# Feed-forward's first quarter: squares on ScalarE, and the first halves of the first two output units ahead of both second halves

## The chip, the cores and the metric

One core of a Trainium2 chip runs the whole program. It has a matrix engine (TensorE, PE in the profile), VectorE (DVE), ScalarE (ACT), GpSimd (POOL) and SyncE (SP), which here only issues DMAs. Each engine takes its instructions in a fixed order that was set when the program was built, and an instruction that waits holds up all that stand behind it on its engine. The metric is the time of one execution on the device, in microseconds (us), as the median of several runs.

## The reference, cut to what matters

Two layers over 640 tokens (128 of a context, 512 latent) and a width of 1024. Each layer has a mixing part (attention and a state-space scan), and behind it a feed-forward part with 4096 hidden units:

```
h = RMSNorm(x) * (1 + scale2) + shift2
x += gate2 * W2 relu(W1 h)^2
```

The change touches only this feed-forward part, in both layers. Its scale, shift and gate differ between context tokens and latent tokens, so operations on a 128x640 tile are often done in two pieces, 128x128 and 128x512.

## The kernel before, in words

The values live transposed: 128 features on the partitions, 640 tokens along the free dimension. A float32 product is made from three: each operand is split into a high part (rounded to the matrix engine's fp32r) and a low part (what is left), and high by high, low by high and high by low are added up in the accumulator. For weights the parts are `wh` and `wl`: ScalarE casts the high one (L1782) and VectorE subtracts for the low one (L1783). For the hidden values they are `uh` and `ul`: a cast on ScalarE (L307) and a subtraction on VectorE (L308).

The hidden units are worked through in four quarters, `q` = 0 to 3, of 8 hidden tiles each. In a quarter, first the **first product** makes 8 hidden tiles of 128x640; then the **second product** runs over 8 output units m = 0 to 7 (128 features of x each), and every unit adds what this quarter's 8 hidden tiles give it. The change is all in q = 0.

- *First product of q = 0.* Tiles 0 and 1 are made together (`early`), tiles 2 to 7 one after the other (`plain`): two `block`s of 24 matmuls on the accumulator `fm`, then `squared`. That multiplies by the norm's factor on VectorE (`un`, L533), copies a small bias vector (`bsh`, L538, ScalarE), adds the bias on ScalarE in two pieces (L1877 and L1878), takes max(v, 0) * v on VectorE (`u`, L1871), and splits it (`uh` on ScalarE, `ul` on VectorE).
- *Second product of q = 0.* Every unit has two blocks. The first reads hidden tiles 0 to 3, the second tiles 4 to 7, which end with the last one made. One block is 4 tiles x 3 products x 2 halves of the tokens, 24 matmuls in 12 groups of two. After its second block a unit's accumulator goes to `residual` (L546), three VectorE operations that add it to x, and so free the accumulator. There are two accumulators of this kind, so unit m + 2 can't begin before unit m's residual is done; `ffx`, the first accumulator of the next quarter, is one of the same two.
- *Beside it.* While the second product of q = 0 runs, VectorE and ScalarE make the operands of the later quarters from x (`expanded`: `nh` L1826 and L1828, `ta` and `tb` L1847, `e`, `eh`, `el`). In layer 0 `fill.step()` puts in work for layer 1's modulation vectors, VectorE multiplications with a throw-away output called `junk` (L428). GpSimd forms sums of weight tiles for the next quarter (`wS`, L1769).
- *Order.* `Stream` hands weights to the blocks in the order of its list `src`, one entry for each block; DMAs run up to seven cost units ahead (an entry costs two here), and the split of the weights is made one block ahead. The order of the instructions on each engine is worked out by the framework's scheduler from the data's dependences and its own estimates, so a change in the code can move instructions elsewhere too.

Of the kernel before, what the change touches and what calls it, by code (L numbers as in the profile page):

```python
# [14 lines left out]
AF = mybir.ActivationFunctionType  # L15
ALU = mybir.AluOpType
# [8 lines left out]
NCTX = 128  # L25
# [80 lines left out]
def build(nc, tc, a, ctx):  # L106
    vec, act, pool, pe = nc.vector, nc.scalar, nc.gpsimd, nc.tensor
# [11 lines left out]
    @contextlib.contextmanager  # L119
    def after(ins):  # L120

        with ExitStack() as st_:
            for i_ in ins:
                st_.enter_context(tc.issue_after(i_.ins))
            yield
# [7 lines left out]
    def nm(s):  # L133
        uid[0] += 1
        return f"{s}_{uid[0]}"
# [7 lines left out]
    def G(shape, dt=F32, name="g"):  # L143

        assert size(shape) <= GW, shape
        return sp.tile(list(shape), dt, tag="G", name=nm(name), bufs=NG)

    def X(shape, dt=F32, name="t"):

        assert size(shape) <= 648, shape  # L150
        return sp.tile(list(shape), dt, tag="X", name=nm(name), bufs=NX)

    def Y(shape, dt=F32, name="t"):

        assert size(shape) <= 512, shape
        return sp.tile(list(shape), dt, tag="Y", name=nm(name), bufs=NXS)
# [4 lines left out]
    def PA(name="pa"):  # L161
        return psp.tile([P, 2, 512], F32, tag="pa", name=nm(name), bufs=2)
# [147 lines left out]
    def halves(ps):  # L310
        return [(ps[:, h, :HT], slice(h * HT, (h + 1) * HT)) for h in range(2)]
# [1430 lines left out]
    class Stream:  # L1742
# [12 lines left out]
        def unit(self, name, cost):  # L1755

            self.src += [(cost, lambda h=h: self.raw(name, h)) for h in range(2)]

        def pair(self, n1, n2):

            box = {}

            def fetch():
                for key, (n, h) in (("11", (n1, 0)), ("21", (n2, 0)), ("22", (n2, 1)), ("12", (n1, 1))):
                    box[key] = self.raw(n, h)
                for key, x0, x1, op in (("S1", "21", "22", ALU.add), ("S2", "S1", "11", ALU.subtract),
                                        ("S3", "11", "21", ALU.subtract), ("S4", "12", "S2", ALU.subtract)):
                    box[key] = Y([P, 512], name="wS")
                    pool.tensor_tensor(out=box[key], in0=box[x0], in1=box[x1], op=op)  # L1769

            def take(key):
                if not box:
                    fetch()
                return box[key]

            self.src += [(1, lambda key=key: take(key)) for key in ("11", "12", "S2", "S1", "S3", "S4", "22")]
# [26 lines left out]
    def block(out, w, xh, xl, first, last, on=False):  # L1803

        hi, lo = w
        with after(done):
            for i in range(4):
                wh, wl = hi[:, i * P:(i + 1) * P], lo[:, i * P:(i + 1) * P]
                for w_, x_, s_, e_ in ((wh, xh[i], first and i == 0, False), (wh, xl[i], False, False),
                                       (wl, xh[i], False, last and i == 3)):  # L1810
                    for o, ts in out:
                        mm = pe.matmul(o, w_, x_[:, ts], start=s_, stop=e_, skip_group_check=on)  # L1812
        done[:] = [mm]
# [38 lines left out]
    def feed_forward(l, nrm, fill):  # L1852
        W = Stream(l)
        for q in range(4):
            if q == 0:
                for m in range(8):
                    W.unit(f"f1_{q}_{m}", 2)
            else:
                for m in range(4):
                    W.pair(f"f1_{q}_{m}", f"f1_{q}_{m + 4}")  # L1860
            for m in range(8):
                W.unit(f"f2_{q}_{m}", 2)
        ex = {n: ([], []) for n in ("B11", "B21", "B22", "T1", "T2", "T3", "T4")}
        expand = expanded(l, nrm, ex)
        nxt = Norm()
        full = slice(0, HT)

        def hidden(v, m, uh, ul):

            u = X([P, T], name="u2")  # L1870
            vec.scalar_tensor_tensor(out=u, in0=v, scalar=0.0, in1=v, op0=ALU.max, op1=ALU.mult)  # L1871
            uh[m], ul[m] = G([P, T], F32R, name="uh"), G([P, T], F32R, name="ul")
            evac_split(uh[m], ul[m], u)

        def squared(m, ps, uh, ul):
            t_, b = nrm.out(ps)
            act.activation(out=t_[:, :NCTX], in_=t_[:, :NCTX], func=AF.Identity, bias=b[:, 0:1])  # L1877
            act.activation(out=t_[:, NCTX:], in_=t_[:, NCTX:], func=AF.Identity, bias=b[:, 1:2])  # L1878
            hidden(t_, m, uh, ul)

        def early(uh, ul):

            ps = [PA("fm") for _ in range(2)]
            ws = [[W.next() for _ in range(2)] for _ in range(2)]
            for k in range(KD):
                with after(nrm.last):
                    if k == 4:
                        nrm.rows()
                    if k == 5:
                        nrm.spread()  # L1890
                for w, p_ in zip(ws, ps):
                    hi, lo = w[k // 4]
                    fm(zhalves(p_), hi[:, (k % 4) * P:], lo[:, (k % 4) * P:], nrm.zh, nrm.zl, [k], 0, KD - 1)
            for m, p_ in enumerate(ps):
                squared(m, p_, uh, ul)

        def plain(m, uh, ul):

            ps = PA("fm")
            for h in range(2):  # L1900
                block(zhalves(ps), W.next(), nrm.zh[4 * h:4 * h + 4], nrm.zl[4 * h:4 * h + 4], h == 0, h == 1)
            squared(m, ps, uh, ul)

        def pair(ms, uh, ul):
            px, pz, py = PA("ffx")[:, 0, :HT], PB("ffz")[:, :HT], PB("ffy")[:, :HT]
            v1, v2_ = X([P, 2, HT], name="v1"), X([P, 2, HT], name="v2")
            sy = Y([P, HT], name="sy")

            def go(out, n, first):
                block([(out, full)], W.next(), *ex[n], first, True, not first)  # L1910

            go(px, "B11", True)
            act.copy(out=v1[:, 0], in_=px)
            go(pz, "B21", True)
            vec.tensor_tensor(out=v1[:, 0], in0=v1[:, 0], in1=pz, op=ALU.add)
            go(px, "T2", False)
            act.copy(out=v1[:, 1], in_=px)
            go(py, "T1", True)
            act.copy(out=sy, in_=py)
            go(px, "T3", False)  # L1920
            vec.tensor_tensor(out=v2_[:, 1], in0=sy, in1=px, op=ALU.add)
            go(py, "B22", False)
            vec.tensor_tensor(out=v1[:, 1], in0=v1[:, 1], in1=py, op=ALU.add)
            go(px, "T4", False)
            act.copy(out=v2_[:, 0], in_=px)
            for v, m in zip((v1, v2_), ms):
                hidden(v.rearrange("p h t -> p (h t)"), m, uh, ul)

        mark(f"{l}ff")
        for q in range(4):  # L1930
            uh, ul = [None] * 8, [None] * 8
            if q == 0:
                early(uh, ul)

                for m in range(8):
                    mark(f"{l}ff")
                    if m >= 2:
                        plain(m, uh, ul)
                    fill.step()
            else:  # L1940
                for m in range(4):
                    mark(f"{l}ff")
                    pair((m, m + 4), uh, ul)
                load_x(xsave, 0)
            for m in range(8):
                mark(f"{l}ff")
                if q and m + 1 < KD:
                    load_x(xsave, m + 1)
                if q == 0 and m < 4:
                    next(expand)  # L1950
                ps = PA("fm")
                for h in range(2):
                    block(halves(ps), W.next(), uh[4 * h:4 * h + 4], ul[4 * h:4 * h + 4], h == 0, h == 1)
                residual(l, 5, m, ps)
                nc.sync.dma_start(a["yT"][:, m] if l == DEPTH - 1 and q == 3 else xsave[:, m], x[m])
                if q == 3:
                    if l + 1 < DEPTH:
                        mark(f"{l + 1}norm1")
                        nxt.scaled(l + 1, 0, m)
                        nxt.square(m)  # L1960
                if q or m >= 4:
                    fill.step()
        while fill.live:
            fill.step()
        return nxt
# [43 lines left out]
    for l in range(DEPTH):  # L2009
        f0 = Part(ada_stream(ADA_S) if l == 0 else ada_rows([(1, 3), (1, 4)]), 1)  # L2010
        n2 = mixing(l, nrm, f0, *((second, raws0) if l == 0 else ()))
# [126 lines left out]
```

## Time and profile before

| | |
|---|---|
| median of 3 runs | 1838.08 us (1836.33 to 1839.86) |
| profiled execution | 1835.58 us |
| its span | 1833.8 us |
| mean granted TensorE clock | 0.968 |
| TensorE busy | 95% of the span |
| VectorE busy | 72% |
| ScalarE busy | 45% |
| GpSimd busy | 25% |

The profiled execution is 2.50 us under the median, and its span 1.78 us shorter than its own time. A share is a mean over the whole span: an engine with a share of 72% can still be full in one stretch, and it is the stretch that counts for a change in one place.

### The profile page before, as it was taken

The numbers are of one execution on the slowest core, as the hardware profiler recorded it, in microseconds if no ns is written. First come the engines' busy times: TensorE is split into PE (matmuls) and PEld (weight loads), VectorE is DVE, ScalarE is ACT, GpSimd is POOL, SyncE is SP. The second block draws the span as 40 slices with busy tenths as digits, with TensorE's granted clock in tenths as the row PEclk, the third lists the DMA queues.
The fourth block names the chain that finished last, engine by engine and source line by source line (L and its number), as shares of the span: only waits on it lengthen the run. The fifth ranks groups of instructions, "written<-read, shape, count | busy, mean of one in ns | idle before, by whom it ended". The sixth has DMA issues, their size and how long they took to land. (4 is left out here: it accounts for less than half of the span.)

```text
span 1833.8 us, 31636 instructions
## 1 busy us (share of the span) xinstructions
PE 1739.1 (95%) x11692; PEld 1616.5 (88%) x11692; DVE 1314.4 (72%) x2738; ACT 828.1 (45%) x1732; POOL 464.3 (25%) x538
## 2 busy tenths in 40 slices
PE   6899998999999999999997999889999999999999
PEld 4797865878999999999997987679989999999998
DVE  6784776744678987786776779988677877465562
ACT  6553446644445351433544533387535445243340
POOL 1424532101210322303135244541003031130400
PEclk8899989999999999999998999789999999999999
DMA  9123122351143447264541322112424242524341
GB/s 337 56 71 101 52 63 80 101 181 64 41 158 107 141 129 231 90 224 133 169 148 45 92 81 85 53 35 75 139 88 138 79 128 86 182 92 157 113 157 57
DMA packets 116588, 209.01 MB, mean 114 GB/s; under 512 B 13393, under 2 KB 28625, under 8 KB 116433
## 3 DMA queue, kind: packets, MB, share of 16 engines
q1 hardware_dynamic: 115872, 206.80, 35.2%
q8 instruction: 92, 1.51, 0.3%
q14 instruction: 64, 0.52, 0.1%
q10 hardware_dynamic: 560, 0.18, 0.0%
HBM read 179.51 MB, written 27.43 MB: 113 GB/s over the span
## 5 line engine op out<-in xcount | busy, mean ns | idle before, releaser
L1782 ACT CAST wh<-wr 128x512 fp32r<-128x512 f32 x232 | 143.6, 621 | 304.9 <-PE fm L1812 193.3
L1812 PE MATMUL fm<-ul,wh 128*128 128x320 f32 x1024 | 235.2, 311 | 10.2 <-DVE ul L308 10.2
L1812 PE MATMUL fm<-uh,wh 128*128 128x320 f32 x1024 | 234.6, 310 | 1.2 <-DVE x L546 1.2
L1812 PE MATMUL fm<-uh,wl 128*128 128x320 f32 x1024 | 234.4, 310 | 0.0
L1783 DVE TENSOR_TENSOR wl<-wr,wh 128x512 fp32r<-128x512 f32 x232 | 179.4, 781 | 75.3 <-issue 41.6
L1769 POOL TENSOR_TENSOR wS<-wr,wr 128x512 f32<-128x512 f32 x48 | 76.1, 1585 | 491.7 <-DMA wr<-in_W 353.9
L1812 PEld LDWEIGHTS fm<-ul,wh 128*128 128x128 f32 x1024 | 172.1, 189 | 11.3 <-DVE ul L308 11.3
L1812 PEld LDWEIGHTS fm<-uh,wh 128*128 128x128 f32 x1024 | 172.4, 189 | 1.6 <-ACT wh L1782 1.4
L1812 PEld LDWEIGHTS fm<-uh,wl 128*128 128x128 f32 x1024 | 172.6, 189 | 0.0
L428 DVE SCALAR_TENSOR_TENSOR junk<-wa,crow 128x512 f32<-128x512 f32 x224 | 155.4, 743 | 4.8 <-DMA wa<-in_w_adaT 4.8
L546 DVE SCALAR_TENSOR_TENSOR x<-fm,mod,x 128x128 f32<-128x128 f32 (+2 forms) x192 | 72.5, 433 | 108.9 <-PE fm L1812 108.9
L1782 ACT CAST wh<-wS 128x512 fp32r<-128x512 f32 x96 | 59.8, 623 | 141.8 <-PE fm L1812 65.7
L766 PE MATMUL tm<-wl,hhi 128*128 128x256 f32 (+2 forms) x400 | 118.2, 296 | 4.9 <-POOL wl L298 4.6
L765 PE MATMUL tm<-wh,hhi 128*128 128x256 f32 (+2 forms) x400 | 118.6, 297 | 3.9 <-DVE zth L786 3.3
L767 PE MATMUL tm<-wh,hlo 128*128 128x256 f32 (+2 forms) x400 | 117.4, 294 | 0.0
L297 ACT CAST wh<-wr 128x512 fp32r<-128x512 f32 (+2 forms) x108 | 66.6, 625 | 72.7 <-PE fm L319 33.1
L1812 PE MATMUL ffx<-eh,wh 128*128 128x320 f32 x288 | 89.3, 310 | 0.0
L1812 PE MATMUL ffx<-eh,wl 128*128 128x320 f32 x288 | 89.0, 309 | 0.0
L1812 PE MATMUL ffx<-el,wh 128*128 128x320 f32 x288 | 88.9, 309 | 0.0
L765 PEld LDWEIGHTS tm<-wh,hhi 128*128 128x128 f32 x400 | 78.3, 196 | 6.1 <-DVE zth L786 4.0
L766 PEld LDWEIGHTS tm<-wl,hhi 128*128 128x128 f32 x400 | 78.4, 196 | 5.8 <-POOL wl L298 4.9
L546 DVE SCALAR_TENSOR_TENSOR x<-wo,mod,x 128x128 f32<-128x128 f32 (+1 forms) x144 | 57.0, 433 | 36.3 <-PE wo L319 34.7
(389 smaller groups left out, 4775.0 us busy)
## 6 DMA issues: line engine op xcount, KB each, us to landing
wr<-in_W SPq DMA_DIRECT2D x351, 256.0 KB, 2.7
wa<-in_w_adaT SPq DMA_DIRECT2D x112, 256.0 KB, 4.4
xsave<-x SPq DMA_DIRECT2D x72, 320.0 KB, 2.2
x<-xsave SPq DMA_DIRECT2D x72, 320.0 KB, 4.2
ws<-in_w_adaS SPq DMA_DIRECT2D x48, 256.0 KB, 4.3
war<-in_w_ada SPq DMA_DIRECT2D x32, 256.0 KB, 5.6
x<-in_xT SPq DMA_DIRECT2D x16, 320.0 KB, 5.4
out_yT<-x SPq DMA_DIRECT2D x8, 320.0 KB, 2.2
```

Source lines behind the costliest of these rows:

```text
L297: act.copy(out=hi[:, :w], in_=raw[:, :w])
L428: vec.scalar_tensor_tensor(out=junk, in0=raws[i], scalar=1.0, in1=row[v][h], op0=ALU.mult, op1=ALU.mult, accum_out=sum_)
L546: vec.scalar_tensor_tensor(out=x[m][:, t0:t0 + n], in0=src, scalar=mods[l][:, j, m, v:v + 1], in1=x[m][:, t0:t0 + n], op0=ALU.mult, op1=AL ...
L765: pe.matmul(ps[:, i, :n], hh[k][:, ts], hi[:, c:c + n], start=s, stop=False)
L766: pe.matmul(ps[:, i, :n], hh[k][:, ts], lo[:, c:c + n], start=False, stop=False)
L767: pe.matmul(ps[:, i, :n], hl[k][:, ts], hi[:, c:c + n], start=False, stop=e)
L1769: pool.tensor_tensor(out=box[key], in0=box[x0], in1=box[x1], op=op)
L1782: act.copy(out=hi, in_=raw)
L1783: vec.tensor_tensor(out=lo, in0=raw, in1=f(hi), op=ALU.subtract)
L1812: mm = pe.matmul(o, w_, x_[:, ts], start=s_, stop=e_, skip_group_check=on)
```

## The change

In q = 0 the two bias additions become a Relu with the same bias, so that the negative part is cut on ScalarE, and the square is taken by a Square on ScalarE in place of the VectorE instruction; 8 tiles in each layer. Then the blocks of output units 0 and 1 are put in another order: first half of unit 0, first half of unit 1, second half of unit 0, second half of unit 1. Both accumulators are held by these two units meanwhile. Units 2 to 7 run as before, and `Stream.two` lists the weights in the new order.

```diff
+        def two(self, n1, n2, cost):
+
+            self.src += [(cost, lambda n=n, h=h: self.raw(n, h)) for h in range(2) for n in (n1, n2)]
...
-            for m in range(8):
+            if q == 0:
+                W.two("f2_0_0", "f2_0_1", 2)
+            for m in range(0 if q else 2, 8):
                 W.unit(f"f2_{q}_{m}", 2)
...
-        def hidden(v, m, uh, ul):
+        def hidden(v, m, uh, ul, pos=False):
 
             u = X([P, T], name="u2")
-            vec.scalar_tensor_tensor(out=u, in0=v, scalar=0.0, in1=v, op0=ALU.max, op1=ALU.mult)
+            if pos:
+                act.activation(out=u, in_=v, func=AF.Square)
+            else:
+                vec.scalar_tensor_tensor(out=u, in0=v, scalar=0.0, in1=v, op0=ALU.max, op1=ALU.mult)
             uh[m], ul[m] = G([P, T], F32R, name="uh"), G([P, T], F32R, name="ul")
             evac_split(uh[m], ul[m], u)
 
         def squared(m, ps, uh, ul):
             t_, b = nrm.out(ps)
-            act.activation(out=t_[:, :NCTX], in_=t_[:, :NCTX], func=AF.Identity, bias=b[:, 0:1])
-            act.activation(out=t_[:, NCTX:], in_=t_[:, NCTX:], func=AF.Identity, bias=b[:, 1:2])
-            hidden(t_, m, uh, ul)
+            act.activation(out=t_[:, :NCTX], in_=t_[:, :NCTX], func=AF.Relu, bias=b[:, 0:1])
+            act.activation(out=t_[:, NCTX:], in_=t_[:, NCTX:], func=AF.Relu, bias=b[:, 1:2])
+            hidden(t_, m, uh, ul, True)
...
-                ps = PA("fm")
-                for h in range(2):
+                if q == 0 and m < 2:
+                    if m == 0:
+                        both = [PA("fm") for _ in range(2)]
+                        for p_ in both:
+                            block(halves(p_), W.next(), uh[:4], ul[:4], True, False)
+                    ps, hs = both[m], (1,)
+                else:
+                    ps, hs = PA("fm"), (0, 1)
+                for h in hs:
                     block(halves(ps), W.next(), uh[4 * h:4 * h + 4], ul[4 * h:4 * h + 4], h == 0, h == 1)
                 residual(l, 5, m, ps)
```

The change lengthens the code above these places, so line numbers behind them differ between the kernels: a block's matmul is L1812 before and L1816 after, the split's subtraction L1783 and L1787, `nh` L1826 and L1830.

Three places in the instruction order of layer 0. The first is TensorE at the start of the second product. Before, the last group of unit 0's first block and its second block up to the low part of the last hidden tile (`ul_6366`; `uh_6365` is its high part, `fm_6415` unit 0's accumulator):

```order
L1812 MATMUL fm_6415<-uh_6025,wl_6330 128x320 x2
L1812 MATMUL fm_6415<-uh_6110,wh_6418 128x320 x2
L1812 MATMUL fm_6415<-ul_6111,wh_6418 128x320 x2
L1812 MATMUL fm_6415<-uh_6110,wl_6419 128x320 x2
L1812 MATMUL fm_6415<-uh_6195,wh_6418 128x320 x2
L1812 MATMUL fm_6415<-ul_6196,wh_6418 128x320 x2
L1812 MATMUL fm_6415<-uh_6195,wl_6419 128x320 x2
L1812 MATMUL fm_6415<-uh_6280,wh_6418 128x320 x2
L1812 MATMUL fm_6415<-ul_6281,wh_6418 128x320 x2
L1812 MATMUL fm_6415<-uh_6280,wl_6419 128x320 x2
L1812 MATMUL fm_6415<-uh_6365,wh_6418 128x320 x2
L1812 MATMUL fm_6415<-ul_6366,wh_6418 128x320 x2
```

Now, from the end of the block that has been put between (unit 1's first half, on its accumulator `fm_6416`) up to the same reading of `ul_6366`:

```order
L1816 MATMUL fm_6416<-uh_6025,wl_6420 128x320 x2
L1816 MATMUL fm_6415<-uh_6110,wh_6449 128x320 x2
L1816 MATMUL fm_6415<-ul_6111,wh_6449 128x320 x2
L1816 MATMUL fm_6415<-uh_6110,wl_6450 128x320 x2
L1816 MATMUL fm_6415<-uh_6195,wh_6449 128x320 x2
L1816 MATMUL fm_6415<-ul_6196,wh_6449 128x320 x2
L1816 MATMUL fm_6415<-uh_6195,wl_6450 128x320 x2
L1816 MATMUL fm_6415<-uh_6280,wh_6449 128x320 x2
L1816 MATMUL fm_6415<-ul_6281,wh_6449 128x320 x2
L1816 MATMUL fm_6415<-uh_6280,wl_6450 128x320 x2
L1816 MATMUL fm_6415<-uh_6365,wh_6449 128x320 x2
L1816 MATMUL fm_6415<-ul_6366,wh_6449 128x320 x2
```

The reading of `ul_6366` has moved from the 23rd group of the second product to the 35th: twelve groups, one block, stand in between that read only hidden tiles 0 to 3.

The second place is VectorE while `ul_6366` is made. Before, from the first instruction behind the last tile's `un_6357` to `ul_6366`:

```order
L1783 TENSOR_TENSOR wl_6545<-wr_6446,wh_6544 128x512
L1783 TENSOR_TENSOR wl_6611<-wr_6512,wh_6610 128x512
L1871 SCALAR_TENSOR_TENSOR u_1496_6363<-un_6357 128x640
L428 SCALAR_TENSOR_TENSOR junk_6369,adares_5846<-wa_6288,crow_5814 128x512
L428 SCALAR_TENSOR_TENSOR junk_6371,adares_5846<-wa_6288,crow_5816 128x512
L428 SCALAR_TENSOR_TENSOR junk_6375,adares_5846<-wa_6294,crow_5815 128x512
L428 SCALAR_TENSOR_TENSOR junk_6377,adares_5846<-wa_6294,crow_5817 128x512
L1826 SCALAR_TENSOR_TENSOR nh_6384<-x_5024,amul_88,nR_5744 128x128
L1826 SCALAR_TENSOR_TENSOR nh_6384<-x_5024,amul_88,nR_5744 128x512
L1826 SCALAR_TENSOR_TENSOR nh_6389<-x_5095,amul_88,nR_5744 128x128
L1826 SCALAR_TENSOR_TENSOR nh_6389<-x_5095,amul_88,nR_5744 128x512
L308 TENSOR_TENSOR ul_6366<-u_1496_6363,uh_6365 128x640
```

Now, from `un_6357` itself:

```order
L533 TENSOR_TENSOR un_6357<-fm_6296,nR_5744 128x640
L1787 TENSOR_TENSOR wl_6545<-wr_6447,wh_6544 128x512
L428 SCALAR_TENSOR_TENSOR junk_6369,adares_5846<-wa_6288,crow_5814 128x512
L428 SCALAR_TENSOR_TENSOR junk_6371,adares_5846<-wa_6288,crow_5816 128x512
L428 SCALAR_TENSOR_TENSOR junk_6375,adares_5846<-wa_6294,crow_5815 128x512
L428 SCALAR_TENSOR_TENSOR junk_6377,adares_5846<-wa_6294,crow_5817 128x512
L1830 SCALAR_TENSOR_TENSOR nh_6384<-x_5024,amul_88,nR_5744 128x128
L1830 SCALAR_TENSOR_TENSOR nh_6384<-x_5024,amul_88,nR_5744 128x512
L1830 SCALAR_TENSOR_TENSOR nh_6389<-x_5095,amul_88,nR_5744 128x128
L1830 SCALAR_TENSOR_TENSOR nh_6389<-x_5095,amul_88,nR_5744 128x512
L1787 TENSOR_TENSOR wl_6611<-wr_6477,wh_6610 128x512
L308 TENSOR_TENSOR ul_6366<-u_1496_6363,uh_6365 128x640
```

The square has left VectorE's queue, and one of the two weight splits stands directly ahead of `ul_6366` now; the four `junk` and the four `nh` are still ahead of it.

The third place is VectorE near the end of the second product, around the residual of unit 6 (`x_5183`), which frees the accumulator for `ffx`. Before:

```order
L1783 TENSOR_TENSOR wl_7048<-wr_6932,wh_7047 128x512
L428 SCALAR_TENSOR_TENSOR junk_7087,adares_6833<-wa_7012,crow_5817 128x512
L546 SCALAR_TENSOR_TENSOR x_5183<-fm_6923,mod_86,x_5183 128x128
L546 SCALAR_TENSOR_TENSOR x_5183<-fm_6923,mod_86,x_5183 128x192
L546 SCALAR_TENSOR_TENSOR x_5183<-fm_6923,mod_86,x_5183 128x320
L1783 TENSOR_TENSOR wl_7114<-wS_6936,wh_7113 128x512
L1783 TENSOR_TENSOR wl_7131<-wS_6934,wh_7130 128x512
```

Now:

```order
L546 SCALAR_TENSOR_TENSOR x_5183<-fm_6923,mod_86,x_5183 128x320
L1787 TENSOR_TENSOR wl_7114<-wS_6936,wh_7113 128x512
L428 SCALAR_TENSOR_TENSOR junk_7010,adares_6833<-wa_6921,crow_5817 128x512
L428 SCALAR_TENSOR_TENSOR junk_7079,adares_6833<-wa_7006,crow_5814 128x512
L428 SCALAR_TENSOR_TENSOR junk_7081,adares_6833<-wa_7006,crow_5816 128x512
L428 SCALAR_TENSOR_TENSOR junk_7085,adares_6833<-wa_7012,crow_5815 128x512
L428 SCALAR_TENSOR_TENSOR junk_7087,adares_6833<-wa_7012,crow_5817 128x512
L1787 TENSOR_TENSOR wl_7131<-wS_6934,wh_7130 128x512
```

Five `junk`, which all stood ahead of this residual, stand behind it now, ahead of the split `wl_7131` that the fourth block of the next quarter reads. Counted from `un_6357` to the last operation of this residual, VectorE has 110 instructions before and 104 now: one square, four `junk` and one weight split fewer.

## Rows read from the trace of the kernel before

**Rows 1.** The page, part 1: busy us (share of the span), instructions.

```profile
PE 1739.1 (95%) x11692; PEld 1616.5 (88%) x11692; DVE 1314.4 (72%) x2738; ACT 828.1 (45%) x1732; POOL 464.3 (25%) x538
```

**Rows 2.** Waits of TensorE, whole program: us, times, longest us.

```profile
PE fm L1812 <- DVE ul L308: 10.2, 4, 3.7
...
PE tm L766 <- POOL wl L298: 4.6, 1, 4.6
```

**Rows 3.** Timeline of TensorE, layer 0: start, us, instruction, [idle before <-releaser].

```profile
570.11 0.46 PE L1812 MATMUL fm<-uh,wh 128*128 128x320 f32 x2
...
576.29 0.46 PE L1812 MATMUL fm<-uh,wh 128*128 128x320 f32 x2
580.42 0.57 PE L1812 MATMUL fm<-ul,wh 128*128 128x320 f32 x2 [3.67 <-DVE ul L308]
...
584.39 0.47 PE L1812 MATMUL fm<-uh,wh 128*128 128x320 f32 x2
```

**Rows 4.** Timeline of TensorE, layer 1, the same place.

```profile
1450.18 0.46 PE L1812 MATMUL fm<-uh,wh 128*128 128x320 f32 x2
...
1456.35 0.45 PE L1812 MATMUL fm<-uh,wh 128*128 128x320 f32 x2
1460.48 0.56 PE L1812 MATMUL fm<-ul,wh 128*128 128x320 f32 x2 [3.68 <-DVE ul L308]
...
1465.04 0.47 PE L1812 MATMUL fm<-uh,wl 128*128 128x320 f32 x2
```

**Rows 5.** Stretches: us, busy us of five engines (PE first), granted clock, DMA.

```profile
582.00:584.00 2.00, 2.00 (x9) 2.00 (x9) 2.00 (x6) 1.62 (x5) 0.00 (x0) 0.50 0.01 4
...
574.00:633.80 59.80, 54.95 (x359) 53.98 (x357) 59.80 (x127) 26.70 (x49) 10.15 (x7) 0.97 0.37 114
```

**Rows 6.** Timeline of VectorE, layer 0, while the last hidden tile is made.

```profile
571.35 0.82 DVE L533 TENSOR_TENSOR un<-fm,nR 128x640 f32<-128x640 f32 x1
...
573.91 0.69 DVE L1783 TENSOR_TENSOR wl<-wr,wh 128x512 fp32r<-128x512 f32 x1 [1.15 <-ACT un L1878]
574.52 0.82 DVE L1871 SCALAR_TENSOR_TENSOR u<-un 128x640 f32<-128x640 f32 x1
575.25 0.68 DVE L428 SCALAR_TENSOR_TENSOR junk<-wa,crow 128x512 f32<-128x512 f32 x1
...
577.70 1.93 DVE L1826 SCALAR_TENSOR_TENSOR nh<-x,amul,nR 128x128 f32<-128x128 f32 x4
579.55 0.82 DVE L308 TENSOR_TENSOR ul<-u,uh 128x640 fp32r<-128x640 f32 x1
```

**Rows 7.** Timeline of ScalarE, the same stretch.

```profile
572.70 0.71 ACT L1878 ACTIVATE un<-un,bsh 128x512 f32<-128x512 f32 x1
...
575.37 0.73 ACT L307 CAST uh<-u 128x640 fp32r<-128x640 f32 x1 [1.19 <-DVE u L1871]
```

**Rows 8.** ScalarE by line and tile: xcount | busy, mean ns | idle before.

```profile
L489 ACT ACTIVATE nsq<-x 128x640 f32<-128x640 f32 x32 | 22.7, 724 | 2.2 <-DVE x L546 2.2
...
L252 ACT ACT_TABLE_LOAD x1 | 1.3, 1283 | 2.2 <-issue 2.2
```

**Rows 9.** Timeline of TensorE, layer 0, end of the second product.

```profile
619.24 0.53 PE L1812 MATMUL fm<-uh,wh 128*128 128x320 f32 x2 [1.18 <-DVE x L546]
...
634.02 0.53 PE L1812 MATMUL ffx<-e,wh 128*128 128x320 f32 x2 [0.21 <-DVE x L546]
```

**Rows 10.** Timeline of TensorE, layer 1, the first matmul on ffx.

```profile
1511.89 0.46 PE L1812 MATMUL ffx<-e,wh 128*128 128x320 f32 x2
```

**Rows 11.** Timeline of VectorE, layer 0: three operations late in the second product.

```profile
590.51 0.48 DVE L1847 TENSOR_TENSOR ta<-nh,ta 128x320 f32<-128x320 f32 x1
...
611.48 1.91 DVE L308 TENSOR_TENSOR el<-nh,eh 128x640 fp32r<-128x640 f32 x1
...
632.75 1.13 DVE L546 SCALAR_TENSOR_TENSOR x<-fm,mod,x 128x128 f32<-128x128 f32 x3
```

**Rows 12.** Timeline of GpSimd, the same stretch.

```profile
611.16 1.54 POOL L1769 TENSOR_TENSOR wS<-wr,wr 128x512 f32<-128x512 f32 x1
```

## The prediction

> **What bounds the kernel now.** I read the shares first: TensorE is busy for 95% of the span, VectorE for 72%, ScalarE for 45% [rows 1]. So time can come only from the stretches in which TensorE stands still or runs at a lower clock, and the second view to read is therefore that of its waits. There, its matmuls on `fm` wait four times for the low part of a hidden tile, 10.2 us in all [rows 2]. The timeline says where the two long ones are: each layer has one of 3.7 us, in the 23rd group of q = 0's second product, which is the first to read the low part of the last hidden tile (I call it tile 7, and output units by their numbers) [rows 3, 4]. The cost of one is more than the wait. A group of two matmuls takes (576.29 - 570.11) / 21 = 0.294 us [rows 3]. From 576.29 to 580.42 it is 4.13 us, 3.84 more than that. Behind the gap the granted clock falls to 0.50 of full speed, the lower of its two levels, 1.2 GHz [rows 5]: the 8 groups from 580.42 to 584.39 take 3.97 us in place of 2.35, 1.62 more. In layer 1 the gap is again 4.13, and the ten groups behind it take 4.56 in place of 2.94, again 1.62 [rows 4]. The place costs 3.84 + 1.62 = **5.46 us in each layer**.
>
> Then I asked VectorE's timeline why tile 7 is late. Its `un` starts at 571.35, its square at 574.52 behind 1.15 us of idling, then four `junk` and four `nh`, and the low part ends at 579.55 + 0.82 = 580.37 [rows 6]: ready 3.8 us after its turn. From 574 to 633.8 VectorE is busy without a break [rows 5], while TensorE waits twice more on residuals: 1.18 us at 619.24 and 0.21 at 634.02 [rows 9]. Layer 0's second product so takes 634.02 - 570.11 = 63.91 us; layer 1's takes 1511.89 - 1450.18 = 61.71 [rows 4, 10], which without its 5.46 is 56.25, what 192 groups of matmuls need. Layer 0 is 7.66 above that. The ceiling of the change is 7.66 + 5.46 = 13.1 us.
>
> **The blocks put in another order.** The 23rd group becomes the 35th. In layer 0 its turn comes at 570.11 + 34 x 0.294 = 580.1. When is the low part of tile 7 ready? A VectorE operation's successor starts 0.08 before its end (577.70 + 1.93 against 579.55 [rows 6]), so I count steps: `un` 0.74, a weight split 0.61, four `junk` 2.45, four `nh` 1.85, another split 0.61, and 0.82 for the low part itself, the order that stands there now. `un` can start when TensorE is through with the first product, one group before 570.11: that group ends at 570.11 - 0.29 + 0.46 = 570.28 [rows 3], with the signal about 570.4. Sum: 570.4 + 7.08 = 577.5. That is 2.6 us before its turn. Before the change `un` started at 571.35 only, with no idle time ahead of it, since VectorE was behind with other work; a square less per tile lets it keep up. The wait goes, and with it the gap from which the clock fell.
>
> **The square on ScalarE.** Removed from VectorE are 8 squares a layer, 16 in all, of 0.82 us each [rows 6]; added to ScalarE are 16 Squares. The same function and shape stands in this kernel in the norm, 0.724 us [rows 8], and I take that. A Relu with a bias doesn't occur; the same instruction with Identity takes 0.71 on 512 columns [rows 7]. Bounds: no cost, and twice that; I take 0.71. The chain of tile 7 on ScalarE: the biases end at 573.41, 1.24 after `un` has ended at 572.17 [rows 6, 7]; now that is 571.2 + 1.24 = 572.5, with 0.72 and 0.73 for the square and the high part 573.9. VectorE reaches the low part only at 576.7, so VectorE's order sets the end, and ScalarE has 2.7 us to spare, more than a doubled Relu and a doubled Square would use (1.4). The other 14 squares stand beside a first product in which these waits don't occur, and are worth nothing to the end. A second function could call for a table load, 1.283 us; the program has one such load in all, with Square and Identity in use [rows 8], and the changed order has one too.
>
> **What is late next: unit 2.** Both accumulators belong to units 0 and 1 for four blocks. Unit 2 begins at group 49, 570.11 + 48 x 0.294 = 584.2, and needs unit 0's residual, which had 7 us of TensorE's work for it before and has one block, 3.5 us, now. Behind the low part (next start 577.4) VectorE has two tiny operations (0.09 each), four of 320 columns (0.48 [rows 11], steps of 0.40), a weight split 0.61, four `nh` 1.86 and a 640-wide split 0.74: 5.0, so 582.4, and the residual of 1.13 [rows 11] ends at 583.5. It fits with 0.7 us to spare, the thinnest margin of this change. ScalarE's casts for these operations wait in part behind weight casts, which need a weight buffer that the blocks free at 577.4 and 580.9; that is inside the same times.
>
> **The end of layer 0's second product.** Here VectorE, not the last tile, sets the end. From `un` at 571.35 to the end of unit 6's residual at 632.75 + 1.13 = 633.88 [rows 6, 11] it takes 62.53 us, 1.15 of it idle. The order now has six instructions fewer up to there: the square (0.73), four `junk` (2.45) and a split (0.61), 3.79. So 62.53 - 1.15 - 3.79 = 57.59, from 570.4 to 628.0, and `ffx` starts at 628.1, 5.9 us earlier. TensorE could be there at 570.11 + 56.25 = 626.4; a wait of some 1.7 us on a residual stays, or comes earlier on units 5 or 6. This sum keeps the stretched operations of before: the same kind of split took 0.82 us mostly and 1.91 at 611.48, while a GpSimd `wS` ran from 611.16 [rows 11, 12]. I count six such operations, 1.1 us each, up to this residual. The Trainium skill ("SBUF — State Buffer", section "Who interferes with whom") says that VectorE and GpSimd share a pair of ports that one of them holds exclusively; this pair of rows agrees, and it would mean that the stretches stay as long as GpSimd's sums stay. Without them the residual would be 6.6 us earlier and no wait would be left.
>
> Behind it five `junk` now stand ahead of the split for the next quarter's fourth block: 628.0 + 0.61 + 3.06 + 0.61 = 632.3, with one or two stretches up to 634.4. Its turn, three blocks of half the size (1.76 each) after `ffx` starts, is 633.4. I take 0.3 of the 0 to 1.0 us. **Layer 0: 5.6.** **Layer 1** has no `junk` there and no residual on which TensorE waited; its whole surplus was the 5.46. The same margins hold, so **5.4**.
>
> **Elsewhere** the new order swaps some neighbours, most in layer 1's mixing part, where one wait of 4.6 us on a GpSimd weight split stands [rows 2]. The bounds are no change and a part of that wait, either way; I take 0, with 1.5 to both sides.
>
> **Sum.** 5.6 + 5.4 = 11.0. The profiled execution of 1835.58 would become 1824.6; it is 2.50 under the median of the runs, and against the median of 1838.08 the result is **1827.1 us**.
>
> **The rivals.** *The whole ceiling:* layer 0's remaining waits go as well, since fewer `junk` stand ahead of each residual and the stretches may fall elsewhere. For it speaks that the waits are small; against it, VectorE's full stretch. 13.1 us, 1825.0. *VectorE's backlog takes the gain:* if all that was moved behind only shifts the same work, layer 0 wins just what VectorE wins, 0.95 of an earlier start, 1.15 of idling and 0.73 of a square, 2.83; with layer 1's 5.4 it is 8.2, 1829.9. For it: no idle time in 60 us. Against: the four `junk` that stand behind the residual now. *A new wait at unit 2 (the one that ends on the other side):* the residual of unit 0 comes late, TensorE stops at group 49, and the clock may fall again. Each microsecond beyond the 0.7 of margin costs one, and a gap like the old one 1.62 more. With 2 us late in both layers it is 3.6 each, and 3.8 of the 11.0 stay: 1834.3. From about 4.5 us beyond the margin in both layers the kernel is slower than before. For it: VectorE is full there, and the residual stands behind five microseconds of work for later quarters. Against: each step of the sum is measured, and 4.5 is nearly as long as that whole work. *The change doesn't do what it says:* the scheduler could have left the low part behind; the order shows it in time, so only if ScalarE is far slower with Relu or Square than its rows.
>
> **How the numbers follow.** Forecast 0.53 (its own range 1825 to 1829.5), whole ceiling 0.13, backlog 0.17, unit 2's wait 0.13, no effect 0.04. The range of 8 in 10 takes in the ceiling with its spread of 1.5, the backlog, and the smaller half of unit 2's wait: 1823.5 to 1832.5. About 0.2% (3.7 us) is what a measurement tells from no change here. Faster by more than that, below 1834.4: the first three and some two fifths of the fourth, 0.88. Within: 0.08. Slower: 0.04.
>
> **What would show it.** Right: no wait on `ul` in the 35th group, no stretch at half clock there, the second product of layer 1 near 56.3 us and that of layer 0 near 58; Squares of 0.72 us and one table load; VectorE's low part of tile 7 near 7.1 us after the end of the first product. Wrong: a wait on the residual at group 49 in either layer, a long wait ahead of `ffx` in layer 0, or time lost in layer 1's mixing part.

## The result, and the profile after

The changed kernel takes 1823.41 us (median of 4 runs, 1820.93 to 1826.74), against 1838.97 us of the kernel before (median of the 4 runs then known, the three shown ahead and one more). The ratio is 0.9914, interval 0.9886 to 0.9941: faster by 10.8 to 21 us. The forecast was 1827.1, between 1823.5 and 1832.5; the measured median lies below that range, by 0.09 us. The profiled execution took 1824.77 us, 1.36 more than the median. Three of all the executions that follow took 2132, 2798 and 7557 us, and are left out of every figure.

The first part of the page after, which answers to [rows 1]:

```profile
PE 1736.3 (95%) x11692; PEld 1615.1 (89%) x11692; DVE 1298.7 (71%) x2722; ACT 837.2 (46%) x1748; POOL 459.0 (25%) x538
```

TensorE is busy for 2.8 us less, though it does the same matmuls (fewer of them run at the lower clock: the mean granted clock is 0.971, and was 0.968); VectorE has 16 instructions less and ScalarE 16 more. The wait of [rows 2] is the place to look at next. The timeline of TensorE after, in layer 0 the first matmul on `fm` with hidden tiles, the first on `ffx`, a wait behind it and the first of the next second product; then the first two of these in layer 1:

```profile
566.76 0.46 PE L1816 MATMUL fm<-uh,wh 128*128 128x320 f32 x2
...
623.19 0.46 PE L1816 MATMUL ffx<-e,wh 128*128 128x320 f32 x2
...
635.56 0.41 PE L1816 MATMUL ffx<-eh,wh 128*128 128x320 f32 x1 [1.45 <-DVE v L1930]
...
674.85 0.45 PE L1816 MATMUL fm<-uh,wh 128*128 128x320 f32 x2
...
1444.72 0.46 PE L1816 MATMUL fm<-uh,wh 128*128 128x320 f32 x2
...
1500.97 0.46 PE L1816 MATMUL ffx<-e,wh 128*128 128x320 f32 x2
```

Layer 0's second product takes 623.19 - 566.76 = 56.43 us in place of 63.91, layer 1's 1500.97 - 1444.72 = 56.25 in place of 61.71. The busy times by stretch say that nothing is left to win there (us, then PE, PEld, DVE, ACT, POOL; the granted clock stands behind them):

```profile
566.80:623.20 56.40, 56.40 (x386) 56.40 (x386) 56.24 (x121) 29.55 (x54) 7.89 (x5) 1.00 0.41 130
1117.00:1134.00 17.00, 14.57 (x67) 11.50 (x65) 16.86 (x33) 5.25 (x9) 6.33 (x6) 0.70 0.08 25
```

In the first of these rows TensorE is busy for all of 56.40 us at the full clock: the waits of [rows 3] and [rows 9] are both gone. (The second row is from layer 1's mixing part and is used below.) But the stretch behind it, the first product of q = 1, takes 674.85 - 623.19 = 51.66 us, and took 683.37 - 634.02 = 49.35 before. Two waits stand in it: 1.45 us on an addition of VectorE (L1930), in the rows above, and 0.20 us on ScalarE (L1922).

VectorE's timeline after, which answers to [rows 6]: `un` of the last tile, the four `nh`, the last low part, and unit 0's residual.

```profile
566.96 0.82 DVE L533 TENSOR_TENSOR un<-fm,nR 128x640 f32<-128x640 f32 x1 [1.94 <-PE fm L1816]
...
570.75 1.94 DVE L1830 SCALAR_TENSOR_TENSOR nh<-x,amul,nR 128x128 f32<-128x128 f32 x4
...
573.20 0.82 DVE L308 TENSOR_TENSOR ul<-u,uh 128x640 fp32r<-128x640 f32 x1
...
578.91 1.13 DVE L546 SCALAR_TENSOR_TENSOR x<-fm,mod,x 128x128 f32<-128x128 f32 x3
```

The last `un` now waits for TensorE (1.94 us); before, VectorE was still busy when it was due [rows 6]. The low part is ready at 573.20 + 0.82 = 574.02, 7.06 us behind the start of `un` (the forecast's steps gave 7.08), and its turn, the 35th group, is at 566.76 + 34 x 0.294 = 576.8. Unit 0's residual ends at 580.04, and unit 2 starts at 566.76 + 48 x 0.2943 = 580.89: a margin of 0.85 us, forecast 0.7. ScalarE in the same stretch (bias with Relu, Square, high part), and its groups in the whole program:

```profile
568.32 0.71 ACT L1887 ACTIVATE un<-un,bsh 128x512 f32<-128x512 f32 x1
569.06 0.74 ACT L1878 ACTIVATE u<-un 128x640 f32<-128x640 f32 x1
569.84 0.73 ACT L307 CAST uh<-u 128x640 fp32r<-128x640 f32 x1
```

```profile
L1878 ACT ACTIVATE u<-un 128x640 f32<-128x640 f32 x16 | 11.8, 740 | 0.6
L1887 ACT ACTIVATE un<-un,bsh 128x512 f32<-128x512 f32 x16 | 11.4, 712 | 0.0
...
L252 ACT ACT_TABLE_LOAD x1 | 1.3, 1283 | 2.2 <-issue 2.2
```

A Relu of 128x512 takes 0.712 us (Identity 0.71 in [rows 7]), a Square 0.740 (0.724 in [rows 8]), and there is still one table load. The high part ends at 569.84 + 0.73 = 570.57, 2.63 us before VectorE starts on the low part (forecast 2.7).

So the profiled execution is 10.8 us shorter than that of before (spans of 1823.0 and 1833.8), and the stretches of the feed-forward that the change touches account for 7.48 - 2.31 + 5.46 = 10.63 of it. The rest nearly cancels here: the program reaches the second product of layer 0 3.35 us earlier (566.76 against 570.11), and loses 3.1 us in layer 1's mixing part. Whether those belong to the change is what the first experiments ask.

### The profile page after: what moved, and what is told of

It reads as the page before. It is cut to its first block, busy times and chain, and to the rows that moved or that the text cites. A ratio compares the mean times of both kernels' runs of the same rounds, so it can differ in the third digit from the quotient of the medians.

```text
span 1823.0 us, 31656 instructions
## 1 busy us (share of the span) xinstructions
PE 1736.3 (95%) x11692; PEld 1615.1 (89%) x11692; DVE 1298.7 (71%) x2722; ACT 837.2 (46%) x1748; POOL 459.0 (25%) x538
## 5 line engine op out<-in xcount | busy, mean ns | idle before, releaser
L1816 PE MATMUL fm<-ul,wh 128*128 128x320 f32 x1024 | 233.9, 309 | 2.9 <-DVE ul L308 2.9
L1816 PE MATMUL fm<-uh,wh 128*128 128x320 f32 x1024 | 233.3, 309 | 0.0
L1816 PE MATMUL fm<-uh,wl 128*128 128x320 f32 x1024 | 233.1, 309 | 0.0
L1787 DVE TENSOR_TENSOR wl<-wr,wh 128x512 fp32r<-128x512 f32 x232 | 177.7, 774 | 71.4 <-issue 42.8
L1816 PEld LDWEIGHTS fm<-ul,wh 128*128 128x128 f32 x1024 | 171.1, 188 | 3.4 <-DVE ul L308 3.4
L1816 PEld LDWEIGHTS fm<-uh,wl 128*128 128x128 f32 x1024 | 171.5, 188 | 0.0
L1816 PEld LDWEIGHTS fm<-uh,wh 128*128 128x128 f32 x1024 | 171.4, 188 | 0.0
L1816 PE MATMUL ffx<-eh,wh 128*128 128x320 f32 x288 | 89.4, 310 | 1.6 <-DVE v L1930 1.4
L1816 PE MATMUL ffx<-el,wh 128*128 128x320 f32 x288 | 89.1, 309 | 0.0
L1816 PE MATMUL ffx<-eh,wl 128*128 128x320 f32 x288 | 89.0, 309 | 0.0
```

The source lines that it names most:

```text
L1787: vec.tensor_tensor(out=lo, in0=raw, in1=f(hi), op=ALU.subtract)
```

## The experiments

The table has the stretches of every trace, each from one first matmul to another in TensorE's timeline: layer 0 from the start (0) to the end of the mixing part (a); the second product of q = 0 (b); the first product of q = 1 (c); the mixing part of layer 1 (d); the second product of q = 0 in layer 1 (e). Behind them stands the ratio of the timed runs to those of before, with its interval.

| kernel | a | b | c | d | e | ratio |
|---|---|---|---|---|---|---|
| before | 506.97 | 63.91 | 49.35 | 432.52 | 61.71 | |
| before, again (e4) | 503.43 | 63.91 | 49.35 | 436.17 | 61.71 | 0.9999 (0.9978 to 1.0019) |
| changed | 503.59 | 56.43 | 51.66 | 435.61 | 56.25 | 0.9914 (0.9886 to 0.9941) |
| changed, again (e1) | 510.68 | 56.43 | 51.61 | 430.66 | 56.25 | 0.9926 (0.9896 to 0.9955) |
| changed, third (e7) | 505.29 | 56.43 | 51.61 | 430.45 | 56.24 | 0.9939 (0.9917 to 0.9961) |
| squares only (e2) | 502.32 | 60.87 | 49.37 | 434.84 | 57.25 | 0.9972 (0.9955 to 0.9988) |
| blocks only (e3) | 505.13 | 63.87 | 49.37 | 437.79 | 61.20 | 1.0001 (0.9983 to 1.0020) |
| changed, junk later (e5) | 503.48 | 56.44 | 49.28 | 432.95 | 56.17 | 0.9908 (0.9884 to 0.9932) |
| changed, Square twice (e6) | 505.67 | 56.43 | 51.79 | 432.05 | 56.24 | 0.9937 (0.9915 to 0.9958) |
| before, junk later (e8) | 505.62 | 61.90 | 49.28 | 437.06 | 62.71 | 0.9985 (0.9965 to 1.0006) |

### What differs between executions: the same two kernels again

No edit: the kernel before and the changed one, timed and traced again.

> The kernel before, unchanged, timed against itself: it shows what a measurement of no change gives (ratio 1.000, with an interval of 0.2 to 0.4% if the spread of the runs is like that of before) and how far the start and layer 1's mixing part differ between two traces of one program. If the starts of two traces of one kernel differ by 2 us or more, the 3.4 us are no part of the change.

> The changed kernel once more, to part what belongs to the change from what differs between executions. In its first trace the start of the program (up to 90 us) is 3.4 us shorter and layer 1's mixing part 3.1 us longer than in the trace of before. Theory A (both are differences between executions; the change is worth what the feed-forward stretches show, 5.2 in layer 0 and 5.5 in layer 1): 10.6 us less than before, ratio 0.9942, and a new trace has another start and another mixing part. Theory B (the new instruction order shortens the start and lengthens the mixing part for good): the same start and the same mixing part again. Theory C (the measured median of 15.6 less is right and the trace doesn't show all of it): ratio near 0.9915. In all: layer 0 from the second product's start to ffx 56.4 us, layer 1 56.3.

> The changed kernel a third time, for the times and for one more trace of the parts outside the feed-forward. Theory A (the feed-forward stretches win 10.65 us in each execution, the rest differs at random by the clock's falls in the mixing parts): feed-forward stretches as before to 0.1 us; the mean of all fast runs of the changed kernel moves towards 10.7 below the mean of before. Theory B (the changed order of layer 1's mixing part wins some 3 to 4 us more): the mean difference stays at 14 to 15 us, and layer 1's mixing part is again near 416 us against 418 to 422 of before.

The feed-forward columns b, c and e agree to 0.05 us between traces of one kernel. The mixing parts do not: three traces of the changed kernel have 503.6, 510.7 and 505.3 us in column a, and 435.6, 430.7 and 430.5 in d. The granted clock falls at places in some executions and not in others: its mean over column a is 0.95, 0.93 and 0.95 in these three traces. The second row of the windows above shows 17 us of layer 1's mixing part at a mean clock of 0.70; in e1's trace the same program has the same place (same tiles, 6.9 us later) at full clock:

```profile
1124.00:1141.00 17.00, 14.31 (x79) 9.86 (x78) 16.97 (x31) 7.67 (x18) 6.68 (x5) 1.00 0.18 58
```

So the 3.4 us at the start needn't belong to the change: two traces of the kernel before differ by 3.5 in the same column. Nor need the 3.1 us lost in layer 1's mixing part: two traces of the changed kernel have gained there (430.7 and 430.5 against 432.5). Theory A holds for the feed-forward stretches. For the whole it is not settled. The 17 runs of the changed kernel in its three comparisons have a mean of 1825.4 us, the 65 of the kernel before one of 1838.7; the difference of 13.3 is uncertain by 2.1 (twice the standard error, from spreads of 3.7 and 4.1), so it is somewhat above the 10.65 of the feed-forward. By such means the gain exceeds that of the stretches by 3.9 us in e5 and 1.3 in e6, which have both parts of the change, and falls short of it by 1.0 in e2 and 0.8 in e3, which have one; each of these is uncertain by 2 to 3 us. The five traces with both parts of the change have a mean of 432.3 in d, the five others of 435.7, but these ranges overlap (430.5 to 435.6, and 432.5 to 437.8), and one program alone spans 5.2. That the changed order of layer 1's mixing part wins 2 to 3 us is possible and not shown.

### The squares alone

```diff
+            if pos:
+                act.activation(out=u, in_=v, func=AF.Square)
...
-            act.activation(out=t_[:, :NCTX], in_=t_[:, :NCTX], func=AF.Identity, bias=b[:, 0:1])
+            act.activation(out=t_[:, :NCTX], in_=t_[:, :NCTX], func=AF.Relu, bias=b[:, 0:1])
...
-            hidden(t_, m, uh, ul)
+            hidden(t_, m, uh, ul, True)
```

The blocks stay in the order of before.

> Squares on ScalarE, blocks in the old order. VectorE's order up to the last low part is that of the changed kernel, so it is ready 7.1 us after the first product's end, and its turn is the 23rd group, about 6.2 to 6.5 us after that end. Theory A (the square alone makes up most of the lateness): a wait of 0.7 to 1.0 us in each layer, no fall of the clock behind it or a short one, gain 4.0 to 4.8 in layer 1, in layer 0 4 to 6.5, in all 8 to 11 us. Rival (only the order hides the last tile; the chain has other waits): the wait stays over 3 us and the gain is under 3 us in all.

TensorE's timeline of this kernel, layer 0 and at the end layer 1:

```profile
574.06 0.56 PE L1812 MATMUL fm<-ul,wh 128*128 128x320 f32 x2 [0.68 <-DVE ul L308]
574.47 0.46 PE L1812 MATMUL fm<-uh,wl 128*128 128x320 f32 x2
...
612.25 0.53 PE L1812 MATMUL fm<-uh,wh 128*128 128x320 f32 x2 [2.06 <-DVE x L546]
...
627.62 0.54 PE L1812 MATMUL ffx<-e,wh 128*128 128x320 f32 x2 [1.03 <-DVE x L546]
...
1453.45 0.56 PE L1812 MATMUL fm<-ul,wh 128*128 128x320 f32 x2 [0.71 <-DVE ul L308]
```

The wait on the last low part is 0.68 and 0.71 us in place of 3.67 and 3.68, and the second group behind it already takes 0.46 us as at full clock: no fall. Layer 1 wins 61.71 - 57.25 = 4.46 us, layer 0 63.91 - 60.87 = 3.04, together 7.5, under the expected 8 to 11, since in layer 0 residuals are waited for at 612.25 and at `ffx` (2.06 and 1.03 us). Theory A holds: the square alone takes away most of the lateness.

### The order of the blocks alone

```diff
-            act.activation(out=t_[:, :NCTX], in_=t_[:, :NCTX], func=AF.Relu, bias=b[:, 0:1])
+            act.activation(out=t_[:, :NCTX], in_=t_[:, :NCTX], func=AF.Identity, bias=b[:, 0:1])
...
-            hidden(t_, m, uh, ul, True)
+            hidden(t_, m, uh, ul)
```

The square is VectorE's again; the blocks stand as in the changed kernel.

> Blocks in the new order, the square left on VectorE with Identity. The low part is ready at the old time, 10.3 us after the start of the second product, and its turn is 10.0 us after it: a wait of 0.3 us. Behind it stand a weight split that waits for the third block, and then unit 0's residual ends some 17 us after the start, while unit 2 begins at 14.1. Theory A: a wait of about 3 us on the residual at unit 2 takes the place of the removed one, with or without the clock's fall, gain 0.5 to 2.5 us in each layer, 1 to 5 in all. Rival (the order alone does it, the square is needed for nothing): no wait at unit 2, gain 9 to 11 us.

TensorE's timeline, layer 0 and then layer 1, and VectorE's in layer 0 (the last low part, four `nh`, a weight split, unit 0's residual in one row with the first operation of unit 1's):

```profile
587.97 0.53 PE L1816 MATMUL fm<-uh,wh 128*128 128x320 f32 x2 [2.73 <-DVE x L546]
...
619.67 0.53 PE L1816 MATMUL fm<-uh,wh 128*128 128x320 f32 x2 [1.72 <-DVE x L546]
...
1474.81 0.54 PE L1816 MATMUL fm<-uh,wh 128*128 128x320 f32 x2 [2.73 <-DVE x L546]
...
1477.53 0.73 PE L1816 MATMUL fm<-ul,wh 128*128 128x320 f32 x2
```

```profile
579.99 0.82 DVE L308 TENSOR_TENSOR ul<-u,uh 128x640 fp32r<-128x640 f32 x1
...
582.62 1.93 DVE L1830 SCALAR_TENSOR_TENSOR nh<-x,amul,nR 128x128 f32<-128x128 f32 x4
...
584.55 0.68 DVE L1787 TENSOR_TENSOR wl<-wr,wh 128x512 fp32r<-128x512 f32 x1
...
586.70 1.38 DVE L546 SCALAR_TENSOR_TENSOR x<-fm,mod,x 128x128 f32<-128x128 f32 x4
```

The wait for the low part is gone (0.17 us of it is left in layer 1), and one of 2.73 us on unit 0's residual stands at unit 2, in both layers. Behind it a group lasts 0.73 us (1477.53) where 0.46 is usual: the lower clock. This is the rival that the prediction put at the margin of 0.7 us: the residual ends some 7 us behind the low part, and the low part is late by a square and what queues up behind it. The second products are 63.87 and 61.20 us; the reorder alone wins nothing (0.04 and 0.51 us by the traces, ratio 1.0001). The mechanism of theory A holds, with a gain below its range.

### ScalarE's cover

```diff
             if pos:
                 act.activation(out=u, in_=v, func=AF.Square)
+                act.activation(out=u, in_=v, func=AF.Square)
```

> The changed kernel with each Square done twice on ScalarE from the same input (0.74 us more for each hidden tile; the result is the same). Theory A (ScalarE has 2.7 us to spare ahead of VectorE at the last tile, and waits in the first product): second products 56.4 and 56.3 us as in the changed kernel, each within 0.4. Rival (the chain over ScalarE bounds the last tile): each layer longer by 0.7 us or more, with a wait on ul or on the high part.

The two groups of Squares on ScalarE in this kernel:

```profile
L1879 ACT ACTIVATE u<-un 128x640 f32<-128x640 f32 x16 | 11.9, 744 | 0.3
L1878 ACT ACTIVATE u<-un 128x640 f32<-128x640 f32 x16 | 11.9, 742 | 0.3
```

12 us more on ScalarE, and columns b and e are the same to 0.01 us: the square is hidden there. Theory A holds.

### The junk in layer 0

```diff
-                if q or m >= 4:
+                if q:
                     fill.step()
```

Once in the changed kernel, once in the kernel before.

> The changed kernel with no fill step (junk) in the second product of the first quarter; the same steps run in the later quarters. In the changed kernel the first pair of the next quarter is 2.3 us longer than before, because three junk that GpSimd's sums stretch to 1.78 us and two more stand ahead of a weight split. Theory A (the gain of layer 0 was partly moved behind ffx, by junk): the first product of the second quarter of layer 0 is 49.4 us again in place of 51.6, the second product before it stays at 56.4, layer 0 wins 2.2 us more, in all about 12.9 us less than before; layer 1 unchanged. Rival (the split is late because of GpSimd's sums themselves, which come early now): 51 to 52 us as in the changed kernel, no gain. Third case: the junk is missing later, the end of layer 0 or the start of layer 1 gets longer by 1 us or more.

> The kernel before with no fill step (junk) in the second product of the first quarter, the same steps run later. It parts the 7.66 us by which layer 0's second product was too long into the last tile's wait and the backlog of VectorE. Theory A (5.46 is the last tile, the other 2.2 are residuals late because of junk and of the operations that GpSimd's sums stretch): layer 0's second product falls from 63.9 to 61.7, the waits on residuals vanish, layer 1 is unchanged at 61.7. Rival (the backlog doesn't come from the junk): 63 us or more.

VectorE in the changed kernel, from unit 6's residual on, and GpSimd beside it:

```profile
620.13 1.13 DVE L546 SCALAR_TENSOR_TENSOR x<-fm,mod,x 128x128 f32<-128x128 f32 x3
...
621.77 0.68 DVE L428 SCALAR_TENSOR_TENSOR junk<-wa,crow 128x512 f32<-128x512 f32 x1
...
622.38 1.78 DVE L428 SCALAR_TENSOR_TENSOR junk<-wa,crow 128x512 f32<-128x512 f32 x1
...
624.09 1.78 DVE L428 SCALAR_TENSOR_TENSOR junk<-wa,crow 128x512 f32<-128x512 f32 x1
...
626.41 1.78 DVE L428 SCALAR_TENSOR_TENSOR junk<-wa,crow 128x512 f32<-128x512 f32 x1
...
631.42 3.69 DVE L1787 TENSOR_TENSOR wl<-wr,wh 128x512 fp32r<-128x512 f32 x3
635.03 0.47 DVE L1930 TENSOR_TENSOR v<-sy,ffx 128x320 f32<-128x320 f32 x1
```

```profile
610.84 1.53 POOL L1773 TENSOR_TENSOR wS<-wr,wS 128x512 f32<-128x512 f32 x1 [8.79 <-DVE junk L428]
621.99 1.62 POOL L1773 TENSOR_TENSOR wS<-wr,wr 128x512 f32<-128x512 f32 x1 [9.61 <-DMA wa<-in_w_adaT]
623.69 1.63 POOL L1773 TENSOR_TENSOR wS<-wS,wr 128x512 f32<-128x512 f32 x1
626.01 1.63 POOL L1773 TENSOR_TENSOR wS<-wr,wr 128x512 f32<-128x512 f32 x1 [0.69 <-issue]
```

Up to unit 6's residual (ended at 621.26) only four of GpSimd's sums have run, where before six had run and a seventh had begun; three more start at 621.99, 623.69 and 626.01, and three of the five `junk` behind that residual take 1.78 us. VectorE is late from there until L1930 at 635.03, for which TensorE waits (635.56 above). With the junk moved to later quarters VectorE waits for TensorE in the same place:

```profile
623.27 1.14 DVE L546 SCALAR_TENSOR_TENSOR x<-fm,mod,x 128x128 f32<-128x128 f32 x3 [2.76 <-PE fm L1816]
...
632.14 0.49 DVE L1930 TENSOR_TENSOR v<-sy,ffx 128x320 f32<-128x320 f32 x1 [1.08 <-PE ffx L1816]
```

Column c falls to 49.28, and b stays at 56.44: the 2.3 us come back, and this kernel, with 7.47 + 0.07 + 5.54 = 13.1 us by its stretches (12.9 expected) and a ratio of 0.9908 (0.9884 to 0.9932), is the fastest of all that ran; the interval of its gain and that of the changed kernel overlap. The end of layer 0 is unchanged. In the kernel before, the junk moved later leaves one wait in layer 0's second product:

```profile
PE fm L1812 <- DVE ul L308: 3.7, 1, 3.7
```

Column b falls to 61.90, as expected (61.7): of the 7.66 us of layer 0, 2.0 belonged to the junk, and the 5.65 that are left to the last tile (5.46 by the prediction). Layer 1 is 62.71 here, 1.0 longer than expected. Its wait is again 3.68 us, but more groups behind it run at the lower clock, the first and the last of them here:

```profile
1461.40 0.90 PE L1812 MATMUL fm<-ul,wh 128*128 128x320 f32 x2 [3.68 <-DVE ul L308]
...
1466.36 0.73 PE L1812 MATMUL fm<-ul,wh 128*128 128x320 f32 x2
```

From 1461.40 to 1466.36 these are ten groups. In e4's trace, at the same place behind the same 3.68 us, the first group lasts 0.90 us too, but only six are slow, and column e is 61.71. The same gap so costs 5.5 or 6.5 us.

## Why the prediction was right and wrong

*The mechanism and its place* were right. The wait for the last low part is gone in both layers with the fall of the clock behind it; the low part is ready 7.06 us after `un` starts (7.08), the residual of unit 0 arrives 0.85 us ahead (0.7), Square and Relu cost what the nearest rows said, and layer 1 wins 5.46 (forecast 5.4).

*The sum for the feed-forward* was right by luck, through two errors that cancel. Layer 0's second product wins 7.48 us, not 5.9. One step that failed is the one that said "this sum keeps the stretched operations of before": six of 1.1 us up to unit 6's residual. The trace of before has these six, one of them in [rows 11] and the others here:

```profile
608.47 1.58 DVE L1847 TENSOR_TENSOR ta<-nh,ta 128x320 f32<-128x320 f32 x1
609.97 1.58 DVE L308 TENSOR_TENSOR e<-nh,e 128x320 fp32r<-128x320 f32 x1
...
615.14 1.57 DVE L1847 TENSOR_TENSOR tb<-nh,ta 128x320 f32<-128x320 f32 x1
...
627.50 1.78 DVE L428 SCALAR_TENSOR_TENSOR junk<-wa,crow 128x512 f32<-128x512 f32 x1
...
630.43 1.78 DVE L1783 TENSOR_TENSOR wl<-wr,wh 128x512 fp32r<-128x512 f32 x1
```

The trace of after has three, each 1.1 us above its kind, since the next sums of GpSimd come behind that residual:

```profile
599.30 1.59 DVE L1851 TENSOR_TENSOR tb<-nh,ta 128x320 f32<-128x320 f32 x1
600.82 1.78 DVE L1787 TENSOR_TENSOR wl<-wr,wh 128x512 fp32r<-128x512 f32 x1
...
611.15 1.77 DVE L428 SCALAR_TENSOR_TENSOR junk<-wa,crow 128x512 f32<-128x512 f32 x1
```

So VectorE took 621.26 - 566.96 = 54.30 us up to there, not 57.59, and the difference of 3.29 is those three operations. They were not saved but moved: on the `junk` behind, where the forecast took 0.3 of 0 to 1.0 us, and 2.3 were lost. Layer 0 so wins 5.2 (5.6), both layers 10.6 (11.0). Both the "whole ceiling" and "backlog" cases came true in part, one behind the other.

*The step from the profiled execution to the median* failed, and this is what put the result outside the range. For the profiled execution the forecast was 1824.6, and it took 1824.77: close, but again by luck, since the 3.35 us that were won ahead of the feed-forward and the 3.1 lost in layer 1's mixing part cancel. The step then added a fixed 2.50, because the execution profiled before "is 2.50 under the median of the runs". This is no property of the program: the profiled execution of the changed kernel is 1.36 us above the median of its runs here, and 4.11 below it in e7. The distance of 3.86 between +2.50 and -1.36, less the 0.17 of the execution itself, is the miss of 3.69 us. Beside it, "elsewhere" was mis-sized: I took 0 with 1.5 to both sides, argued from the instruction order alone. What the runs showed in its place is that the parts outside the feed-forward differ by up to 7 us between executions of one program, much of it by the clock's falls, so that a median of four runs has a standard error of some 2 us (an estimate from the runs' spread of 3.7). The mean of the 17 runs, 1825.4, lies inside the range: the four of the result came out low by chance in part. Whether 2 to 3 us were won outside the feed-forward stays open.

*The rival at unit 2* was real: without the squares on ScalarE it takes nearly the whole gain (e3). The two parts of the change need each other, the order to hide the last 0.7 us and the square to bring the residual in time: 7.5 us and 0.5 us alone, 10.6 together. In layer 0 the order does one thing more: with the squares alone, VectorE still has six stretched operations ahead of unit 6's residual, and TensorE waits for residuals (2.06 and 1.03 us, e2); with both parts these waits are gone.

## What to carry to other kernels

A reorder that gives a late tile more time also gives something else less: count, for the accumulator that is held longer, when its release is due, and what stands on that engine's queue ahead of it. Work that is taken off a full engine is worth most where the chain passes, and two edits at one place are not the sum of their gains: try each alone. Before you give a range for a change of half a percent, look at how far two traces of the same program differ, stretch by stretch, and compare kernels by the stretches that the change touches. Don't carry the distance of one profiled execution from the median of its runs over to another kernel.

## What the runs showed of the hardware that was not expected

Whether the granted clock falls is not fixed by the program: the same 17 us of layer 1's mixing part ran at a mean clock of 0.70 in one execution and 1.00 in another, and column a differs by 7.1 us between two traces of the changed kernel. In these second products waits of 0.7, 1.7 and 2.1 us were followed by the full clock (e2, e3), those of 2.7 and 3.7 by a fall to 0.50, the lower level of 1.2 GHz, in every trace in which they stood; the price behind the same wait of 3.68 us was 1.6 us in layer 1 of both traces of the kernel before and 2.6 in e8. Each of VectorE's stretched operations beside a GpSimd sum is 1.1 us longer, whether it is a `junk`, a split or a difference, so where the sums fall decides which wait they feed.
